# Batch norm with ReLU: the four parameter vectors read by the gpsimd queue in place of the scalar queue

## The chip, the core and the metric

The kernel runs on one core of one Trainium2 chip. A core has a matrix engine (PE, TensorE), a vector engine (DVE), a scalar engine (ACT), a general engine (POOL, GpSimd) and a sync engine (SP) that here only issues transfers. Each of them works through its own queue of instructions, and they wait for one another by semaphores. Transfers between the chip's main memory (HBM) and the on-chip memory (SBUF) are issued by an engine's queue and carried out by 16 DMA engines.

The metric is the time in microseconds (us) that the device takes for one execution. The kernel before takes 84.79 us, the median of 4 runs (84.65 to 84.92).

## The reference

The input `x` is a float32 array of 32 x 128 x 32 x 32 (16.78 MB), and the output has the same shape. Each of the 128 channels has four parameters, so that the vectors `gamma`, `beta`, `running_mean` and `running_var` are 512 bytes each.

```python
normalized = (x - running_mean[None, :, None, None]) / np.sqrt(running_var[None, :, None, None] + eps)
scaled = normalized * gamma[None, :, None, None] + beta[None, :, None, None]
return np.maximum(scaled, 0).astype(np.float32)
```

## The kernel before

The 4096 planes (32 batches x 128 channels) of 1024 floats are laid out so that each of the 128 partitions holds 16 consecutive planes at a time (`J = 16`), in two rounds. Each round is split in two pieces of 8 planes, so there are four tiles `x` of 128 x 8192 floats, 4 MB each. Every tile has a buffer of its own, and no buffer is used twice.

**Loads (L50).** SP's queue issues the four loads of `x` one after the other, with nothing to wait for.

**Parameters (L55 to L88).** The tile `raw` has 8 partitions, with 4 x 16 floats in each: partition q holds the 16 channels from 16q on, of the variance, gamma, mean and beta. Four reads of 512 bytes fill it (L57), issued by the scalar engine's queue. POOL makes a matrix `rep` of 8 x 128 with a memset (L61) and a select (L62); it has a one where the column's number modulo 8 is the row's number. One matmul (L72, carried out as two passes) multiplies the two and so spreads `raw` over all 128 partitions into `cols`. It waits for `rep` and for all four reads. ACT takes the square root of the variance plus `eps` (L80; it loads its function table first, and this load stands in its queue behind the four reads), and DVE makes the reciprocal (L82), `scale_t` (L84), the product with the mean (L86) and `bias_t` (L88).

**Work and stores (L90 to L99).** For each tile, in the order of loading, ACT runs eight activations `Relu(scale * x + bias)` in place, one for each plane (L92), and SP issues the tile's store (L99), which waits for the last of the eight. Loads and stores thus stand in one queue of transfers, SP's, in the order of their issue.

**Order and semaphores.** The order on each engine is that of the program, engine by engine; the waits are put in by the framework. It deals out semaphores for transfers in turn: eight for those of SP and ACT together. In the kernel before, twelve transfers share them: the variance's read has the first, the first load the second, the reads of gamma, mean and beta the third to fifth, the other loads the sixth to eighth, and the four stores the first to fourth again. At the end of the program (its instructions are shown at L130) SP goes through a list of waits for all semaphores in use, two in each instruction; in the kernel before there are five such instructions, and the one with the last store's semaphore is the first of them. Then a drain and two meetings of all engines follow, with POOL's clearing of the semaphores between them. The instructions of the start are shown at L116.

Of the kernel before, what the change touches and what calls it, by code (L numbers as in the profile page):

```python
# [1 line left out]

# [4 lines left out]


F32 = mybir.dt.float32
ACTF = mybir.ActivationFunctionType  # L10

J = 16

PIECES = ((0, 8), (8, 16))


@with_exitstack
def kernel(  # L20
    ctx: ExitStack,
    tc: tile.TileContext,
    x: bass.AP,
    gamma: bass.AP,
    beta: bass.AP,
    running_mean: bass.AP,
    running_var: bass.AP,
    eps: bass.AP,
    out: bass.AP,
):  # L30
    nc = tc.nc
    B, C, H, W = x.shape
    HW = H * W
    P = nc.NUM_PARTITIONS
    assert C % J == 0 and P % (C // J) == 0 and (B * C) % (P * J) == 0
    Q = C // J
    T = B * C // (P * J)

    xr = x.rearrange("b c h w -> (b c) (h w)").rearrange("(t p j) w -> t p j w", p=P, j=J)
    outr = out.rearrange("b c h w -> (b c) (h w)").rearrange("(t p j) w -> t p j w", p=P, j=J)  # L40

    data = ctx.enter_context(tc.tile_pool(name="data", bufs=1))
    params = ctx.enter_context(tc.tile_pool(name="params", bufs=1))
    psum = ctx.enter_context(tc.tile_pool(name="psum", bufs=1, space=bass.MemoryType.PSUM))

    tiles = []
    for t in range(T):
        for a, b in PIECES:
            xt = data.tile([P, b - a, HW], F32, name=f"x{t}_{a}")
            nc.sync.dma_start(out=xt, in_=xr[t, :, a:b, :])  # L50
            tiles.append((t, a, b, xt))

    raw = params.tile([Q, 4, J], F32, name="raw")  # L55
    for k, src in enumerate((running_var, gamma, running_mean, beta)):
        nc.scalar.dma_start(out=raw[:, k, :], in_=src.rearrange("(q j) -> q j", j=J))  # L57
    eps_t = params.tile([P, 1], F32, name="eps_t")
    nc.vector.memset(eps_t, float(eps))  # L59
    rep = params.tile([Q, P // Q, Q], F32, name="rep")  # L60
    nc.gpsimd.memset(rep, 1.0)  # L61
    nc.gpsimd.affine_select(  # L62
        out=rep,
        in_=rep,
        compare_op=mybir.AluOpType.is_equal,
        fill=0.0,
        base=0,
        pattern=[[0, P // Q], [-1, Q]],
        channel_multiplier=1,
    )  # L70
    cols = psum.tile([P, 4, J], F32, name="cols")
    nc.tensor.matmul(  # L72
        cols.rearrange("p k j -> p (k j)"),
        rep.rearrange("q r s -> q (r s)"),
        raw.rearrange("q k j -> q (k j)"),
        start=True,
        stop=True,
    )
    std_t = params.tile([P, J], F32, name="std_t")
    nc.scalar.activation(out=std_t, in_=cols[:, 0, :], func=ACTF.Sqrt, bias=eps_t[:, 0:1], scale=1.0)  # L80
    rstd_t = params.tile([P, J], F32, name="rstd_t")
    nc.vector.reciprocal(out=rstd_t, in_=std_t)  # L82
    scale_t = params.tile([P, J], F32, name="scale_t")
    nc.vector.tensor_mul(out=scale_t, in0=cols[:, 1, :], in1=rstd_t)  # L84
    ms_t = params.tile([P, J], F32, name="ms_t")
    nc.vector.tensor_mul(out=ms_t, in0=cols[:, 2, :], in1=scale_t)  # L86
    bias_t = params.tile([P, J], F32, name="bias_t")
    nc.vector.tensor_sub(out=bias_t, in0=cols[:, 3, :], in1=ms_t)  # L88

    for t, a, b, xt in tiles:  # L90
        for j in range(a, b):
            nc.scalar.activation(  # L92
                out=xt[:, j - a, :],
                in_=xt[:, j - a, :],
                func=ACTF.Relu,
                bias=bias_t[:, j : j + 1],
                scale=scale_t[:, j : j + 1],
            )
        nc.sync.dma_start(out=outr[t, :, a:b, :], in_=xt)  # L99


# [1 line left out]
_INS = ['x', 'gamma', 'beta', 'running_mean', 'running_var', 'eps']  # L103
_OUTS = [((32, 128, 32, 32), 'float32')]

_NUMBERS = {'eps': 1e-05}


# [26 lines left out]
```

## Time and profile before

| what | us |
| --- | --- |
| median of 4 runs | 84.79 (84.65 to 84.92) |
| the profiled execution | 84.86 |
| its span, first to last instruction | 83.1 |
| ACT busy, of this the 32 activations of L92 | 38.0, 36.4 |
| mean of one activation of L92 | 1.226 |
| PE, DVE, POOL busy | 0.7, 0.8, 0.8 |
| SP's queue issues the four loads | 0.80 to 2.70 |
| ACT's queue issues the four parameter reads | 0.80 to 2.43 |
| the matmul starts | 13.04 |
| ACT's first activation of L92 starts | 15.03 |
| stores are issued, first and last | 24.21, 52.54 |

The span is the time between the first and the last instruction that the profiler saw; the run's own time has 1.76 us more around it. A line of the profile names the line of the kernel, the engine, the operation, the tile written and the tile read. The rows with a q after the engine's name (ACTq, SPq) are instructions of its queue, such as the issue of a transfer. Their duration is that of the issue, not of the transfer. The row that is called DMA gives, for each of 40 slices of the span, the busy share of the 16 DMA engines in tenths.

Below the views stand the records that they are made of: each packet of a transfer with its queue, start, duration and size, and each change of a semaphore with its time. Where a transfer's landing is given with its time, it is that of the last change of its semaphore by a DMA engine. The packets are not marked with the engine that carried them.

### The profile page before, as it was taken

To read this page: it belongs to the slowest core of one execution; us is meant where nothing else is said; L and a number is where in the kernel's file an instruction comes from. 1 tells how busy PE (TensorE), PEld (TensorE's weight loads), DVE (VectorE), ACT (ScalarE), POOL (GpSimd) and SP (SyncE) were. 2 spreads that over 40 slices of the span, in tenths; PEclk is the share of its full clock that TensorE was granted. 3 is DMA by queue.
4 is the path that set the end of the run, shared out by engine and by line. 5 is a ranking of instruction groups with operands and counts; after the bars stand their busy time and mean duration, and the time that the engine had idled before them with its cause. 6 is when DMAs were issued, how large, how long until landed. Compare 5 with 4: busy or idle time off the path is not lost.

```text
span 83.1 us, 115 instructions
## 1 busy us (share of the span) xinstructions
PE 0.7 (1%) x2; PEld 0.5 (1%) x2; DVE 0.8 (1%) x5; ACT 38.0 (46%) x34; POOL 0.8 (1%) x6
## 2 busy tenths in 40 slices
PE   0000003000000000000000000000000000000000
PEld 0000002000000000000000000000000000000000
DVE  0000001100000000000000000000000000000000
ACT  0600001799999999999949999200000000000000
POOL 3000000000000000000000000000000000000000
DMA  7779996997999699899769998998999899899980
GB/s 205 300 315 442 505 457 300 504 504 315 441 504 473 284 504 504 347 410 504 252 284 473 489 410 363 504 426 378 457 504 394 363 504 473 363 426 504 410 347 0
DMA packets 1216, 33.56 MB, mean 404 GB/s; under 512 B 192, under 2 KB 192, under 8 KB 192
## 3 DMA queue, kind: packets, MB, share of 16 engines
q1 hardware_dynamic: 1152, 33.55, 95.7%
q10 hardware_dynamic: 64, 0.00, 0.0%
HBM read 16.78 MB, written 16.78 MB: 404 GB/s over the span
## 4 chain that ended last, share of the span: by engine, by line
DMA 50%; ACT 10%; SPq 1%; ACTq 1%; issue 0%
DMA x<-in_x_dram 50%; ACT x L92 10%; SPq L50 1%; ACTq L130 1%
## 5 line engine op out<-in xcount | busy, mean ns | idle before, releaser
L92 ACT ACTIVATE x<-x,bias_t,scale_t 128x1024 f32<-128x1024 f32 x32 | 36.4, 1226 | 2.1 <-DMA x<-in_x_dram 1.1
L80 ACT ACTIVATE std_t<-cols,eps_t 128x16 f32<-128x16 f32 x1 | 0.3, 274 | 9.9 <-PE cols L72 9.9
L80 ACT ACT_TABLE_LOAD x1 | 1.3, 1283 | 2.5 <-issue 2.5
L72 PE MATMUL cols<-raw,rep 8*128 8x64 f32 x2 | 0.7, 428 | 13.0 <-DMA raw<-in_beta_dram 13.0
L72 PEld LDWEIGHTS cols<-raw,rep 8*128 8x128 f32 x2 | 0.5, 308 | 13.0 <-issue 13.0
L62 POOL TENSOR_SCALAR_AFFINE_SELECT rep<-rep 8x128 f32<-8x128 f32 x1 | 0.4, 392 | 0.1
L82 DVE RECIPROCAL rstd_t<-std_t 128x16 f32<-128x16 f32 x1 | 0.3, 253 | 13.1 <-ACT std_t L80 13.1
L61 POOL MEMSET rep<- 8x128 f32 x1 | 0.2, 195 | 0.3 <-POOLq L116 0.3
L86 DVE TENSOR_TENSOR ms_t<-cols,scale_t 128x16 f32<-128x16 f32 x1 | 0.2, 174 | 0.0
L88 DVE TENSOR_TENSOR bias_t<-cols,ms_t 128x16 f32<-128x16 f32 x1 | 0.2, 174 | 0.0
L84 DVE TENSOR_TENSOR scale_t<-cols,rstd_t 128x16 f32<-128x16 f32 x1 | 0.2, 173 | 0.1
L116 POOL MEMSET const-uint8-127<- 128x1 uint8 x1 | 0.1, 107 | 0.0
L116 POOL MEMSET const-float32-0.0<- 128x1 f32 x1 | 0.1, 104 | 0.3 <-issue 0.3
L116 POOL MEMSET const-bfloat16-1.0<- 128x1 bf16 x1 | 0.1, 106 | 0.0
L116 POOL MEMSET const-float32-1.0<- 128x1 f32 x1 | 0.1, 103 | 0.0
L59 DVE MEMSET eps_t<- 128x1 f32 x1 | 0.1, 59 | 0.9 <-PEq L116 0.9
## 6 DMA issues: line engine op xcount, KB each, us to landing
x<-in_x_dram SPq DMA_DIRECT2D x4, 4096.0 KB, 26.0
out_dram<-x SPq DMA_DIRECT2D x4, 4096.0 KB, 29.4
raw<-in_running_var_dram ACTq DMA_DIRECT2D x1, 0.5 KB
raw<-in_gamma_dram ACTq DMA_DIRECT2D x1, 0.5 KB
raw<-in_running_mean_dram ACTq DMA_DIRECT2D x1, 0.5 KB
raw<-in_beta_dram ACTq DMA_DIRECT2D x1, 0.5 KB
```

The costliest lines, as they stand in the source:

```text
L50: nc.sync.dma_start(out=xt, in_=xr[t, :, a:b, :])
L61: nc.gpsimd.memset(rep, 1.0)
L62: nc.gpsimd.affine_select(out=rep, in_=rep, compare_op=mybir.AluOpType.is_equal, fill=0.0, base=0, pattern=[[0, P // Q], [-1, Q]], channel ...
L72: nc.tensor.matmul(cols.rearrange("p k j -> p (k j)"), rep.rearrange("q r s -> q (r s)"), raw.rearrange("q k j -> q (k j)"), start=True, s ...
L80: nc.scalar.activation(out=std_t, in_=cols[:, 0, :], func=ACTF.Sqrt, bias=eps_t[:, 0:1], scale=1.0)
L82: nc.vector.reciprocal(out=rstd_t, in_=std_t)
L84: nc.vector.tensor_mul(out=scale_t, in0=cols[:, 1, :], in1=rstd_t)
L86: nc.vector.tensor_mul(out=ms_t, in0=cols[:, 2, :], in1=scale_t)
L88: nc.vector.tensor_sub(out=bias_t, in0=cols[:, 3, :], in1=ms_t)
L92: nc.scalar.activation(out=xt[:, j - a, :], in_=xt[:, j - a, :], func=ACTF.Relu, bias=bias_t[:, j : j + 1], scale=scale_t[:, j : j + 1],)
L116: nc = _bacc.Bacc("TRN2", target_bir_lowering=False, num_devices=1)
L130: with _tile.TileContext(nc) as tc:
```

## The change

The four reads of the parameter vectors are issued by the gpsimd engine's queue (POOL) in place of the scalar engine's. Sources, destination and order stay the same.

```diff
     raw = params.tile([Q, 4, J], F32, name="raw")
     for k, src in enumerate((running_var, gamma, running_mean, beta)):
-        nc.scalar.dma_start(out=raw[:, k, :], in_=src.rearrange("(q j) -> q j", j=J))
+        nc.gpsimd.dma_start(out=raw[:, k, :], in_=src.rearrange("(q j) -> q j", j=J))
     eps_t = params.tile([P, 1], F32, name="eps_t")
```

In the built program, the four transfers stand on POOL ahead of the memset of `rep` (L61) and the select (L62). On ACT the table load is now the first instruction of the work. PE, DVE and SP have the same instructions in the same order, with other semaphores: the four reads have four semaphores of another group, which belongs to POOL's transfers, and the loads and stores have the eight of SP and ACT to themselves, the loads the first four and the stores the last four. SP's closing list has seven instructions in place of five, with the last store's semaphore in the seventh, and POOL clears a range of 20 semaphores in place of 12.

## The prediction

> **What bounds the kernel now.** I read the page's head first (span, DMA rows, queues), then the waits of the sync engine's queue, then the timeline of the head, then the packet and semaphore records that the trace keeps below these views.
>
> ```profile
> span 83.1 us, 115 instructions
> ...
> PE 0.7 (1%) x2; PEld 0.5 (1%) x2; DVE 0.8 (1%) x5; ACT 38.0 (46%) x34; POOL 0.8 (1%) x6
> ...
> DMA  7779996997999699899769998998999899899980
> ...
> q1 hardware_dynamic: 1152, 33.55, 95.7%
> q10 hardware_dynamic: 64, 0.00, 0.0%
> ```
>
> No engine is busy for half the span, while the transfers on SP's queue (q1) fill 95.7% of sixteen DMA engines' time. The four parameter reads (q10) are 64 packets and no visible share. In the packet records, q1 is 1,024 packets of 32 KB, and nearly all take 1.213 us: 64 for each of 16 engines, 64 x 1.213 = 77.6 us that nothing but fewer bytes can shorten. The rest of the span is a head (the first packets start at 1.80 to 2.42 and take 1.90 on average), a slow turn from reading to writing, and a tail.
>
> ```profile
> SPq L99 <- ACT x L92: 37.4, 4, 11.1
> SPq L130 <- DMA out_dram<-x: 29.2, 1, 29.2
> ```
>
> SP's last wait is 29.2 us long and for the last store: that store, issued at 52.54, lies behind stores issued long before. By the semaphore records the loads land at 13.10, 22.6, 32.3 and 43.34, the stores at 53.0, 62.7, 72.4 and 82.06, one each 9.7 us. So ACT does not set the end: it only has to hand over each tile before the rings run dry.
>
> ```profile
> 0.80 0.58 ACTq L57 DMA_DIRECT2D raw<-in_running_var_dram  x1
> 0.80 0.20 POOL L61 MEMSET rep<- 8x128 f32 x1 [0.29 <-POOLq L116]
> 0.80 1.90 SPq L50 DMA_DIRECT2D x<-in_x_dram  x4
> ...
> 2.52 1.28 ACT L80 ACT_TABLE_LOAD   x1 [2.52 <-issue]
> ...
> 13.04 0.66 PE L72 MATMUL cols<-raw,rep 8*128 8x64 f32 x2 [13.04 <-DMA raw<-in_beta_dram]
> ...
> 15.03 27.25 ACT L92 ACTIVATE x<-x,bias_t,scale_t 128x1024 f32<-128x1024 f32 x24 [1.02 <-DVE bias_t L88]
> ```
>
> The parameters land at 12.91 (beta's semaphore) though they were issued by 2.43: an engine that has work on both queues takes one small packet, then one of x, so each DMA's data packet and its increment cost a turn of 1.213 us each. PE starts at 13.04, ACT's first Relu at 15.03, only 1.9 after its tile landed.
>
> ```profile
> L130 SPq EVENT_SEMAPHORE  x5: 28/28/28, 82.1 to 82.3; - x5
> L130 SPq DRAIN  x1: 7/7/7, 82.4 to 82.4; - x1
> ```
>
> These are SP's closing waits. The records have them at 82.073, 82.142, 82.204, 82.268 and 82.330, the drain at 82.395: one each 64 ns. The first of them holds the last store's semaphore, so the other four run after the last byte, on the path.
>
> **The change, part by part.**
>
> *Removed from ACT's queue:* four issues of 584, 277, 318 and 358 ns. ACT's table load moves from 2.52 to about 0.9. It is worth nothing: ACT then waits until 13 for the matmul either way.
>
> *Added to POOL's queue*, ahead of the memset (195 ns) and the select (392 ns) that make `rep`. No row shows an issue from POOL. From below, ACT's 277 ns each: 4 x 0.28 = 1.1 us. From above, the longest instruction of the head, the 1.28 us table load: 4 x 1.28 = 5.1 us. I take 0.8 each, between them. `rep`, ready at 1.47 now, is ready between 2.6 and 6.6, at 4.7 by my value. PE waits for `raw` long after that, so nothing of it shows.
>
> *The parameters' landing.* An engine has read ahead in q1 by the time a small packet comes: gamma, issued at 1.41, got its first turn at 6.12, behind three packets of x. Low: turns from 6.12, and one turn a transfer if data and increment go in one packet: 6.12 + 3 x 1.216 + 0.36 (12.55 of beta's last turn to 12.91) = 10.1. High: the last issue at 5.9, 1.0 to its first packet (as from 0.80 to 1.80 for x), three packets of read-ahead, 8 turns: 5.9 + 1.0 + 3.6 + 9.7 = 20.2. I take eight turns from 6.12, the nearest to what stands there now, since only the variance's early two turns are lost: 6.12 + 7 x 1.216 + 0.36 = 15.0. ACT's first Relu, 2.1 after it (15.03 - 12.91) and not before the tile at 13.10, is then at 17.1 (13.1 to 22.3). What is late next? The first store, issued at 24.21, 9.2 after the first Relu, goes to 26.3 (22.3 to 31.5). It has to be there when the first engine leaves its loads: first packet done at 3.70, 31 more end at 41.3; less three packets of read-ahead (3.6) and 1.0 from issue to packet, 36.7. That leaves 10 us of cover by my value and 5 at the high end; later stores have more, since ACT needs 9.1 per tile and the engines 9.7. With the cover gone each further us would cost one. Value: 0.
>
> *The first load's issue.* SP's first issue of x takes 373 ns beside ACT's, the four stores, alone, 332 to 348. Without ACT's beside it x may start 0.03 earlier, and everything follows. From both sides: 0, and the 0.62 by which the first packets' starts are spread (1.80 to 2.42), if all of that spread came from sharing. The four parameter issues are short and touch 8 engines only; I take 0.03.
>
> *What the small packets cost the engines.* Now: 1.216 between x packets with a small one between, 1.213 without, 3 ns x 8 turns = 24 ns. Afterwards, descriptors come by another path, of which the trace shows nothing: from -0.024 (free) to, if each engine pays one start like its first packet's, 1.904 - 1.213 = +0.69. I take 0, since the rows of small packets are nearest.
>
> The Trainium skill speaks against the change here. *DMA: Bandwidth & Descriptors*, section "Latency and other measured facts", says that engines 7 and 15 are usually slower, with a best guess that software-made descriptors' rings share their ports. In this trace the last store's 16 increments arrive evenly from 81.43 to 82.06, and no two stand apart. The page gives no price; any would go straight to the end. The same page's specifications give about 1 us to the first byte from gpsimd and 0.6 from scalar (the trace: 0.95 from the variance's issue to its first packet); by that the landing would be 0.4 later, and the sum the same.
>
> *The closing waits.* The scheduler now has other semaphores. Before, all twelve DMAs shared eight, so the last store reused an early one and stands in the first of five waits. After, the parameter reads have four of their own and the stores the last four of eight; the built program has seven waits on SP, and the last store's semaphore in the seventh. The six others pass while the store is under way. So of 338 ns from landing (82.057) to drain (82.395), 16 + 65 = 81 stay: -0.257. From both sides: -0.257, and 0 if something else holds the drain. POOL's range clear at the end takes 20 semaphores for 12: 12 are cleared in 47 ns (82.782 to 82.829), 8 more make +0.031.
>
> Sum: -0.257 + 0.031 - 0.033 + 0 = -0.26. The profiled execution took 84.86 (span 83.1 and 1.76 around it) and would take 84.60; the median of the runs, 84.79, becomes 84.53.
>
> **The rivals.**
>
> *The head gains more* (83.94): the whole spread of the starts, 0.62, goes, with the tail: 84.79 - 0.226 - 0.62. For it: every SP issue of x beside an ACT issue is longer (373 to 530) than a store's. Against: the last starters need not be engines that carry parameters, and POOL's issues may crowd in the same way.
>
> *It eats itself up* (84.79): the new packets cost the engines the 0.26 that the tail gives, 0.26 / 8 = 33 ns a turn where 3 are paid now. For it: four more increments on idle engines; against: the small packets last only 9 to 11 ns.
>
> *A stall of the engines* (85.2, slower): the engine that turns to the software-made descriptors waits for them while x waits behind. One place: the turns between 4 and 14 us; one price: 0.69 per stall, as the first packets; 84.53 + 0.69 = 85.22, four stalls (one for each read) 87.3. It decides from 0.26 + 0.25 = 0.51 in all, 64 ns a turn. For it: the load phase has no slack anywhere. Against: a ring with x in it is never empty, and today's turns cost 3 ns.
>
> *The reads are hidden anyway* is no rival but the ground of the forecast; that they land 10 us later than I say, past 25, would be a slower case, beyond the high end of 20.2.
>
> **How the numbers follow.** No change means within 0.3%, 0.25 us, which is about what a measurement of this kernel can tell: 84.54 to 85.04. The forecast (0.58, own range 84.35 to 84.70) lies on that edge: 0.33 faster, 0.25 same. The larger head gain has 0.10, all faster. The one that eats itself up has 0.10: 0.08 same, 0.02 slower. The stall has 0.22, all slower. Together 0.43, 0.33, 0.24. The range runs from 84.15, which cuts off the upper half of the head's gains, to 85.4, past one stall.
>
> **What would show it.** SP's closing waits: one, not five, between the last landing and the drain. Small packets on a POOL queue of another kind, their neighbours still 1.216 apart. The first x packets' starts against 1.80 to 2.42. Last loads' landing at 43.3 and stores each 9.7. It is wrong if packets of x stand further apart between 4 and 14, if time around the span grows, or if the first Relu begins after 27.

## The result and the profile after

The changed kernel takes 84.63 us (median of 43 runs, 84.49 to 84.84), against 84.83 for the kernel before in the same comparison (64 runs, 84.56 to 84.99). The ratio is 0.998, with a 95% interval of 0.9975 to 0.9985. It is faster, but by 0.2 us only. The profiled execution took 84.67 us, 1.70 us more than its span, which is 82.97 us in the records; before it was 1.71 us more than 83.15 (the 1.76 given ahead of the prediction comes from the span rounded to 83.1). So nearly all of the difference lies in the span.

The head of the page, with the busy times, the DMA rows and the queues:

```profile
span 83.0 us, 117 instructions
...
PE 0.7 (1%) x2; PEld 0.5 (1%) x2; DVE 0.8 (1%) x5; ACT 37.9 (46%) x34; POOL 3.0 (4%) x10
...
DMA  5989988998999899899769979998997999899790
...
q1 hardware_dynamic: 1152, 33.55, 95.7%
q0 software_dynamic: 128, 0.00, 0.1%
```

SP's transfers fill the same 95.7%. The four reads are now 128 packets of a queue of another kind in place of 64: the records have 16 changes of each read's semaphore by DMA engines, and 32 packets for each read, so that all 16 engines seem to take part, with two packets each. POOL is busy for 2.2 us more, and that is the issue of the reads, as the timeline shows:

```profile
0.82 2.01 SPq L50 DMA_DIRECT2D x<-in_x_dram  x4
...
1.03 1.28 ACT L80 ACT_TABLE_LOAD   x1 [1.03 <-DVE eps_t L59]
1.33 0.67 POOL L57 DMA_DIRECT2D raw<-in_running_var_dram  x1 [0.81 <-POOLq L116]
2.00 0.52 POOL L57 DMA_DIRECT2D raw<-in_gamma_dram  x1
2.51 0.52 POOL L57 DMA_DIRECT2D raw<-in_running_mean_dram  x1
3.02 0.52 POOL L57 DMA_DIRECT2D raw<-in_beta_dram  x1
...
14.48 0.66 PE L72 MATMUL cols<-raw,rep 8*128 8x64 f32 x2 [14.48 <-DMA raw<-in_beta_dram]
...
16.47 36.30 ACT L92 ACTIVATE x<-x,bias_t,scale_t 128x1024 f32<-128x1024 f32 x32 [1.02 <-DVE bias_t L88]
25.65 27.48 SPq L99 DMA_DIRECT2D out_dram<-x  x4
```

The parameters arrive later: the matmul starts 1.44 us later than before and the first Relu too. What is late next is the first store, issued at 25.65 in place of 24.21. There it ends: ACT now runs all 32 activations without a stop, as it no longer catches up with the fourth load (before, it waited 1.08 us for it), and the stores land at 53.04, 62.72, 72.40 and 82.07, where they landed at 53.03, 62.70, 72.39 and 82.06.

The end of SP's queue, first the waits that took longest, then the closing instructions between 82.05 and 82.18:

```profile
SPq L130 <- DMA out_dram<-x: 28.6, 3, 9.6
```

```profile
L130 SPq EVENT_SEMAPHORE  x1: 28/28/28, 82.1 to 82.1; - x1
L130 SPq DRAIN  x1: 7/7/7, 82.2 to 82.2; - x1
```

The one long wait of 29.2 us has become three, one for each of the last stores, so that most of the list is done before the last byte lands. One wait is left behind it where there were five. In the records the drain starts 0.082 us after the last landing (82.068 to 82.150); before, it was 0.338.

### The profile page after: what moved, and what is told of

Same layout as the page of the kernel before. It is cut to its first block, busy times and chain, and to the rows that moved or that the text cites. A ratio compares the mean times of both kernels' runs of the same rounds, so it can differ in the third digit from the quotient of the medians.

```text
span 83.0 us, 117 instructions
## 1 busy us (share of the span) xinstructions
PE 0.7 (1%) x2; PEld 0.5 (1%) x2; DVE 0.8 (1%) x5; ACT 37.9 (46%) x34; POOL 3.0 (4%) x10
## 3 DMA queue, kind: packets, MB, share of 16 engines
q1 hardware_dynamic: 1152, 33.55, 95.7%
## 4 chain that ended last, share of the span: by engine, by line
ACT 43%; DMA 14%; POOL 2%; ACTq 1%; issue 1%; DVE 1%; PE 1%; DVEq 0%; POOLq 0%
ACT x L92 42%; DMA raw<-in_beta_dram 14%; POOL raw L57 2%; ACTq L130 1%; PE cols L72 1%; ACT std_t L80 0%; DVE rstd_t L82 0%; DVE ms_t L86 0%; DVE bias_t L88 0%; DVE scale_t L84 0%; DVEq L84 0%; POOLq L116 0%
## 5 line engine op out<-in xcount | busy, mean ns | idle before, releaser
L57 POOL DMA_DIRECT2D raw<-in_running_var_dram x1 | 0.7, 672 | 0.8 <-POOLq L116 0.8
L57 POOL DMA_DIRECT2D raw<-in_beta_dram x1 | 0.5, 521 | 0.0
L57 POOL DMA_DIRECT2D raw<-in_gamma_dram x1 | 0.5, 518 | 0.0
L57 POOL DMA_DIRECT2D raw<-in_running_mean_dram x1 | 0.5, 518 | 0.0
L62 POOL TENSOR_SCALAR_AFFINE_SELECT rep<-rep 8x128 f32<-8x128 f32 x1 | 0.4, 397 | 0.1
L61 POOL MEMSET rep<- 8x128 f32 x1 | 0.2, 194 | 0.0
```

The lines of the kernel that those rows point to most:

```text
L57: nc.gpsimd.dma_start(out=raw[:, k, :], in_=src.rearrange("(q j) -> q j", j=J))
L62: nc.gpsimd.affine_select(out=rep, in_=rep, compare_op=mybir.AluOpType.is_equal, fill=0.0, base=0, pattern=[[0, P // Q], [-1, Q]], channel ...
```

## The experiments

Eleven runs were made: eight further kernels, one of which ran twice, and the changed kernel twice more. Each was timed against the kernel before on the same chip, and the ratios have 95% intervals. Three numbers sort them: where the last store lands, how long the program goes on after it, and the median.

| kernel | last landing | from there to the end | median | ratio to before |
| --- | --- | --- | --- | --- |
| before | 82.06 | 1.09 | 84.83 | 1 |
| changed | 82.07 | 0.90 | 84.63 | 0.998 (0.9975 to 0.9985) |
| ACT's queue, four copies more | 81.91 | 0.83 | 84.47 | 0.9968 (0.9955 to 0.9981) |
| the same again | 81.87 | 0.83 | 84.49 | 0.9961 (0.9947 to 0.9975) |
| POOL's queue, four copies more | 82.04 | 1.15 | 84.84 | 1.0003 (0.9993 to 1.0013) |
| no reads | 81.95 | 0.83 | 84.55 | 0.9972 (0.9962 to 0.9982) |
| POOL's queue, reads late | 82.09 | 0.90 | 84.68 | 0.9991 (0.9982 to 0.9999) |
| changed, second run | 81.95 | 0.90 | 84.62 | 0.9972 (0.9962 to 0.9983) |
| changed, third run | 82.06 | 0.90 | 84.63 | 0.9981 (0.9969 to 0.9994) |
| reads behind the second load | 82.02 | 1.09 | 84.77 | 0.9992 (0.9983 to 1.0001) |
| reads behind the third load | 84.56 | 1.09 | 87.42 | 1.0305 (1.0291 to 1.0318) |
| stores halved by planes | 82.22 | 0.83 | 84.79 | 0.9993 (0.9984 to 1.0002) |
| stores halved by partitions | 111.64 | 0.83 | 114.12 | 1.3437 (1.339 to 1.3483) |

The second column comes from one profiled execution each, and scatters by some 0.1 us between runs of one kernel. The third does not: it is the same to 0.001 us in all three runs of the changed kernel.

**Reads on ACT's queue, closing waits as in the changed kernel.** Four small copies on ACT's queue bring the transfers to sixteen, so that the last store gets the last of the eight semaphores.

```diff
             )
+        if t == 0 and a == 0:
+            spare = params.tile([Q, 4, J], F32, name="spare")
+            for k in range(4):
+                nc.scalar.dma_start(out=spare[:, k, :], in_=xt[0:Q, 7, 0:J])
         nc.sync.dma_start(out=outr[t, :, a:b, :], in_=xt)
```

> The kernel before (reads on ACT's queue) with four more transfers: ACT copies 64 bytes from each of 8 partitions of the first finished tile into a tile that nobody reads. Sixteen transfers share the eight semaphores, so the last store's stands in the last of SP's five closing waits, as in the changed kernel, and the clear at the end still takes 12 semaphores. Theory (the gain is the order of the closing waits): last landing near 82.06 as before, 0.08 us from there to the drain in place of 0.34, so 84.83 - 0.26 + 0.02 for the copies' packets = 84.59, ratio 0.997. Rival (the gain comes from the path of the reads or the relief of ACT's queue): 84.83 or above, ratio 1.000.

It took 84.47 us, 0.9968. The closing instructions between 81.9 and 82.0:

```profile
L134 SPq EVENT_SEMAPHORE  x1: 28/28/28, 81.9 to 81.9; - x1
L134 SPq DRAIN  x1: 7/7/7, 82.0 to 82.0; - x1
```

Again one wait is left. The gain comes without any change to the queue of the reads. It is 0.1 us more than the theory had, and that part lies in the landing, at 81.91 here: a side effect or scatter of the start, which this run does not tell apart. One thing besides the copies differs: the third and fourth load share semaphores with gamma and mean, and SP issued them only at 7.95 and 10.39, well before the rings (what the DMA engines have in their queues) needed them. In this profile and in that of the same kernel run again, the second load lands at 22.53 and 22.48 against 22.62 before, ahead of the copies, which are issued from 24.1 on (24.0 in the second), and the fourth at 43.20 and 43.17 against 43.34. So at least half of this lead is not the copies' doing; whether it comes from the late issue of the two loads is open.

**Reads on POOL's queue, closing waits as before.** The same copies in the changed kernel, where twelve transfers now share the eight semaphores and the last store gets the fourth.

```diff
-        nc.scalar.dma_start(out=raw[:, k, :], in_=src.rearrange("(q j) -> q j", j=J))
+        nc.gpsimd.dma_start(out=raw[:, k, :], in_=src.rearrange("(q j) -> q j", j=J))
...
+                nc.scalar.dma_start(out=spare[:, k, :], in_=xt[0:Q, 7, 0:J])
```

> The changed kernel (reads on POOL's queue) with the same four copies on ACT's queue. Twelve transfers now share the eight semaphores of SP and ACT, so the last store's stands in the third of seven closing waits with four behind it, as many as before. Theory (closing waits): 0.34 us from the last landing to the drain and the wider clear, 0.07, still paid: 84.83 + 0.07 = 84.90, ratio 1.001. Rival (path of the reads): the gain stays, 84.63, ratio 0.998.

It took 84.84 us, 1.0003: the gain is gone, with the reads on POOL's queue. The closing instructions between 82.0 and 82.4:

```profile
L134 SPq EVENT_SEMAPHORE  x5: 28/28/28, 82.1 to 82.3; - x5
L134 SPq DRAIN  x1: 7/7/7, 82.4 to 82.4; - x1
```

The five waits are back, and the drain starts 0.328 after the landing. With the run before, this makes a table of two by two: reads on ACT or POOL, list short or long. The list decides in both rows.

This kernel goes on for 1.15 us after the landing, 0.06 longer than the kernel before with its five waits. That is POOL's part of the end, first before, then here:

```profile
L130 POOLq DRAIN  x3: 34/82/486, 1.0 to 82.9; - x3
L130 POOLq EVENT_SEMAPHORE_RANGE_CLEAR  x1: 96/96/96, 82.8 to 82.8; - x1
```

```profile
L134 POOLq DRAIN  x3: 40/102/10544, 3.7 to 82.9; - x3
L134 POOLq EVENT_SEMAPHORE_RANGE_CLEAR  x1: 139/139/139, 82.8 to 82.8; - x1
```

The clear takes 139 ns for 20 semaphores and 96 for 12, and the drains around it 102 and 40 for 82 and 34 (the long third drain of each line lies in the head). The changed kernel, with the same wider clear, goes on for 0.821 us after its drain has started, against 0.752 before: 0.07 us.

**No reads.** This leaves out the reading of the four vectors; DVE fills the tile with ones and zeros.

```diff
-    for k, src in enumerate((running_var, gamma, running_mean, beta)):
-        nc.scalar.dma_start(out=raw[:, k, :], in_=src.rearrange("(q j) -> q j", j=J))
+    nc.vector.memset(raw[:, 0:2, :], 1.0)
+    nc.vector.memset(raw[:, 2:4, :], 0.0)
```

> No parameter reads at all: DVE fills the tile of parameters with ones and zeros, which leaves out the reading of the four vectors. Eight transfers, so the last store's semaphore stands in the last of five closing waits; the clear takes 12 semaphores. Theory (closing waits alone, the reads cost the DMA engines and the head next to nothing): 84.83 - 0.26 - 0.02 = 84.55, ratio 0.9967. Rival (the reads hold up the first packets of x on either path, the head can gain): first packets done clearly before 3.9 and 84.1 to 84.4.

It took 84.55 us, 0.9972, as the theory said. The first packets of x start at 1.80 to 2.40 and are done at 3.48 to 3.99 (before: 1.80 to 2.42 and 3.70 to 4.05). So there is next to nothing to win in the head by moving the reads, wherever they go.

**POOL's reads after the first packets.** In the first profile of the changed kernel one engine's increments came 0.28 us after those of all others, in every transfer, most likely because its first packet was done at 4.27 where the other fifteen were done by 4.02 (an increment is the step by which each of the 16 engines raises a transfer's semaphore when its part is done).

```diff
+    hold = params.tile([P, 4096], F32, name="hold")
+    nc.gpsimd.memset(hold, 0.0)
     for k, src in enumerate((running_var, gamma, running_mean, beta)):
```

> The changed kernel with a long memset of an unused tile on POOL ahead of the four reads, so that POOL issues them only after about 5 us, when each DMA engine is past its first packet of x. In the changed kernel's profile one engine ended its first packet 0.25 us after all others and ended last by as much. Theory 1 (POOL's issues at 1.3 to 3.5 hold up that engine): its lag goes, the 16 increments of the last store end together, 84.63 - 0.25 = 84.38, ratio 0.995. Theory 2 (such a lag is chance, of the first packets themselves): 84.63 within 0.08, ratio 0.998. The first Relu at 18 to 21 is covered either way.

POOL's timeline:

```profile
0.81 3.51 POOL L57 MEMSET hold<- 128x4096 f32 x1 [0.29 <-POOLq L118]
...
4.26 0.67 POOL L59 DMA_DIRECT2D raw<-in_running_var_dram  x1
...
16.62 0.66 PE L74 MATMUL cols<-raw,rep 8*128 8x64 f32 x2 [16.62 <-DMA raw<-in_beta_dram]
```

The reads were issued from 4.26 on and the first Relu was at 18.61. The time was 84.68, no faster than the changed kernel's 84.63. The first theory falls: keeping POOL away from the first packets gains nothing.

**The changed kernel again**, twice, as it is.

> The changed kernel once more, for its landings. Theory (the engine that lagged by 0.25 us in its first profile is chance): the 16 increments of the last store end together, last landing between 81.85 and 82.1, median 84.63, ratio 0.998. Rival (POOL's transfers hold up one engine each time): one increment again 0.2 to 0.3 after the other fifteen in each transfer.

> The changed kernel, for comparison with the run before. Theory: 84.62, ratio 0.9975, 0.07 above the kernel with the copies, and the last store's increments without one engine apart. Rival: at or below it.

They took 84.62 and 84.63, and their ratios hold the first one's. In the second run the last two increments of the last store came together at 81.937 and 81.952, but 0.18 after the one ahead of them (81.754). In the third the last came at 82.055, 0.17 after the one ahead, in the kernel before at 82.057, 0.125 after. So it is not one engine by 0.28 each time, and the lag scatters. Whether POOL's queue has a small part in it is open: in the four profiles with POOL's reads at the start (the one of POOL's queue with four copies has 0.19) the last one or two engines stand 0.17 to 0.28 apart, in the others, but for the stores halved by partitions, by 0.15 at most. Holding the reads back, at any rate, gained no time.

> Reads on ACT's queue with the four small copies once more, beside the changed kernel on one chip. Theory (both have the short closing list, this one without the wider clear): 84.55, 0.07 below the changed kernel. Rival (POOL's queue has an advantage of its own): the changed kernel is the faster one.

Beside the third run, on one chip, the kernel with the reads on ACT's queue and the short list took 84.49 and the changed one 84.63. POOL's queue has no advantage of its own. The gap of 0.14 is twice the price of the wider clear; the rest is again in the landing (81.87 and 82.06 in the two profiled executions, which lie further apart than the medians).

**How late the parameters may come.** The reads go to SP's own queue, behind the second load or, with a 3 in place of the 2, behind the third. ACT's queue issues none.

```diff
             tiles.append((t, a, b, xt))
+            if len(tiles) == 2:
+                for k, src in enumerate((running_var, gamma, running_mean, beta)):
+                    nc.sync.dma_start(out=raw[:, k, :], in_=src.rearrange("(q j) -> q j", j=J))
```

> The four reads stand on SP's own queue behind its second load, so that they land when that load does, near 22.7 in place of 12.9; twelve transfers, closing waits as before. Theory (cover of the reads ends when the first store is issued later than about 36.7): first Relu at 24.8, first store at 34.0, no change: 84.83, ratio 1.000 within 0.002. Rival (the reads' landing is on the path to some degree, so what the changed kernel won or lost came from it): slower in proportion to 9.8 us of delay, at least 0.3 us.

> The same with the reads behind the third load: landing near 32.4, first Relu at 34.5, first store at 43.7. Theory (cover ends at 36.7, each us past it costs one): 7.0 us slower, 91.8. Rival (only the time counts in which the rings are truly empty, from the end of the last load's packets near 41.6 to the first store's packet, 1.0 after its issue): 3.1 us slower, 87.9, or 86.7 if the slow turn from reading to writing, 1.2, goes with it.

Behind the second load, the first Relu is at 25.29 and the first store at 34.47, 10.3 us later than before, and the time is 84.77: covered. Behind the third it is 87.42. Its DMA row, and the DMA engines' busy share by stretches (the last two columns are the share and the GB/s):

```profile
DMA  7697999989997999799009995999599969998890
```

```profile
40.00:42.00 2.00, 0.00 (x0) 0.00 (x0) 0.00 (x0) 2.00 (x3) 0.00 (x0) 1.00 0.46 197
42.00:44.00 2.00, 0.00 (x0) 0.00 (x0) 0.00 (x0) 2.00 (x2) 0.00 (x0) 1.00 0.00 0
44.00:46.00 2.00, 0.00 (x0) 0.00 (x0) 0.00 (x0) 2.00 (x3) 0.00 (x0) 1.00 0.61 262
```

The two zeros in the row are the price: from the end of the loads' last packet, at 41.58, to the first store's packets at 45.09, no engine has work. That is 3.5 us, but the last landing is only 2.50 later than before (84.56 and 82.06). The packets around the turn from reading to writing, which in the kernel before took 1.19 us per engine more than their 1.213 each, have no such excess here (0.01), while the stores' packets take 0.2 us more in all for each engine. The theory's 91.8 is missed by far, and the rival's 86.7 to 87.9 holds: the cover ends later than I had put it, and past its end a microsecond counts only while the rings are empty.

**A version that needs no superfluous transfer.** Halved stores also make sixteen transfers, first by planes, then by partitions.

```diff
-        nc.sync.dma_start(out=outr[t, :, a:b, :], in_=xt)
+            if (j - a) % 4 == 3:
+                nc.sync.dma_start(out=outr[t, :, j - 3 : j + 1, :], in_=xt[:, j - 3 - a : j + 1 - a, :])
```

> The kernel before, with reads on ACT's queue, and each tile stored in two halves of four planes: sixteen transfers and nothing superfluous, so that the last store's semaphore is in the last of five closing waits, and the clear takes 12 semaphores. Theory (closing waits): 0.08 from last landing to drain, end 0.83 after the landing: 84.83 - 0.26 = 84.57, ratio 0.997, less than the changed kernel by the narrower clear, 0.07, if packets of 16 KB run at the rate of those of 32 KB. Rival (half as large packets cost each engine some ns apiece, 32 more per engine): 3 ns each takes 0.1 back, 8 ns all of it, 84.83.

It took 84.79 us, 0.9993. The end is as short as it should be (0.83), but the last store lands at 82.22: a packet of 16 KB takes 0.611 us, two of them 1.222 where one of 32 KB takes 1.213. 32 pairs for each engine make 0.29 us, about what the short list had given. Less than that shows: the last landing is 0.17 later than before, and the median 0.05 below that of the kernel before beside it (84.84).

```diff
-        nc.sync.dma_start(out=outr[t, :, a:b, :], in_=xt)
+        for p in (0, P // 2):
+            nc.sync.dma_start(out=outr[t, p : p + P // 2, a:b, :], in_=xt[p : p + P // 2])
```

> The kernel before, reads on ACT's queue, each tile stored in two halves of 64 partitions, so that the packets stay at 32 KB (the halves by planes had packets of 16 KB at 0.611 us, 9 ns more for each pair). Sixteen transfers, the last store's semaphore in the last of five closing waits. Theory (closing waits, and packets of 32 KB at 1.213): 84.83 - 0.26 = 84.57, ratio 0.997. Rival (half of the partitions is half of the memory's width, and the store's packets take longer): packets over 1.3 us and well above 85.

This took 114.12 us. By stretches of the load and the store phase:

```profile
6.00:34.00 28.00, 0.66 (x2) 0.50 (x2) 0.78 (x4) 19.40 (x18) 0.00 (x0) 1.00 1.00 433
46.00:110.00 64.00, 0.00 (x0) 0.00 (x0) 0.00 (x0) 6.56 (x6) 0.00 (x0) 1.00 0.96 237
```

The engines are as busy as ever, but the stores move 237 GB/s where the loads move 433: in that stretch a store's packet of 32 KB takes 2.45 us at the median, twice the usual 1.213, though a quarter of the stores' packets still take 1.25 or less. The Trainium skill, in *DMA: Bandwidth & Descriptors*, section "Rules for kernel authors", advises against transfers to disjoint halves of the partitions, since they share the same engines and serialize. This case agrees that it does not help, and shows more: from the last load's landing to the last store's it is 68.3 us in place of 38.7. The rival's forecast, packets over 1.3 us and a time well above 85, is the one that held; why the packets are slower, no run here shows.

Of all these the kernel with the reads on ACT's queue and four small copies is the fastest, 84.47 and 84.49. It beats both kernels, the changed one by 0.14 us beside it.

## Why the prediction was right

Faster was forecast, by 0.26 us to 84.53; it is faster by 0.20. The mechanism is the one that was forecast, the closing waits, and the experiments show it. The terms, against what was measured:

- *Closing waits*, -0.257: from landing to drain 0.338 before and 0.082 after, -0.256. Shown by the table of two by two: the short list gives the gain with reads on ACT's queue, and the long list takes it away with reads on POOL's.
- *The wider clear*, +0.031: it is +0.07. I had worked from the times at which the semaphores change, 12 in 47 ns. The instruction itself takes 139 ns for 96, and the drains around it some more. This is half of what the sum missed.
- *The first load's issue*, -0.033: nothing. Without ACT's issue beside it, it takes 383 ns (378 and 376 in the other runs), where it took 373. With no reads at all, the four issues of x take 376, 425, 424 and 519 ns, where they took 373, 427, 424 and 530 beside ACT's. So the difference from the stores' 332 to 348 is not the price of sharing. The rival of a larger head gain falls with it: the first packets start at 1.83 to 2.48 now, no closer together than at 1.80 to 2.42, and the kernel with no reads has much the same head.
- *The small packets*, 0: right. There are twice as many of them, and the gap between two packets of x with a small one between stays at 3 ns at the median. The stall of the engines did not come.
- *The landing of the parameters*, 15.0, first Relu 17.1, first store 26.3, and no cost: 14.35, 16.47 and 25.65, and no cost. The first turn was at 6.08, as forecast at 6.12, but seven turns passed and not eight: beta's landing follows mean's by 1.20 us, one turn, where the others follow by 2.44 and 2.47. POOL's issues take 0.67 and 0.52, not 0.8, and begin at 1.33. The cover was put at 36.7 for the first store; the store issued at 34.47 costs nothing, the one at 44.22 costs 2.5, and the end between these two was not tried. An estimate from the second of these runs, whose engines end their loads at 41.14 to 41.58 and whose first store has its first packets 0.86 us after its issue, puts the end near 40.3 to 40.7.

Without the head's term and with the clear at its measured price the sum is -0.256 + 0.07 = -0.19, which is 84.64 from the comparison's 84.83, against 84.63. The result lies within 0.3% of the time before, the half of the forecast's case that had the smaller chance, because two small terms were each some hundredths off and the forecast stood on that edge. The edge of 0.25 us was put at what a measurement of this kernel can tell, and that was too wide: the interval of the ratio is 0.001 wide, which is 0.08 us.

One reading of the prediction was loose, and nothing in the sum rests on it: the last store's increments before do not arrive quite evenly, as the last stands 0.125 us behind the one ahead of it (81.932 and 82.057).

## What to carry to other kernels

An instruction that moves from one queue to another can change which semaphore each later transfer gets, and so what stands behind the last landing: read the list of closing waits in the built program beside the instructions that the diff names. Where the DMA engines are full from end to end, ask of every other step only how late it may come before their rings run empty; here the parameters had more than 10 us. Changes of this size are told from scatter by the part of the span that repeats (here 0.902 to 0.903 us in three runs), from the last landing to the end, and not by the landing itself.

## What was not expected of the hardware

The turn from reading to writing cost 1.19 us for each engine in the kernel before, where the last loads and the first stores overlap, and 0.01 where a pause lay between them. Stores of 64 partitions moved most of their packets at half the rate of those of 128 (2.45 against 1.213 us for 32 KB, at the median). And the four reads from POOL's queue are 128 packets, where ACT's were 64. Each read has 8 packets of 64 bytes and 24 of 4 bytes, as if the engines that carry none of the data took two packets of 4 bytes. The Trainium skill, in *DMA: Bandwidth & Descriptors*, section "Why a DMA increments its semaphore by 16 and not by 1", has all 16 engines post their increment on this path, which fits the 16 changes of each read's semaphore here; why there are two packets, no run here shows.
